# Left-operand blocks of a two-layer decoder trunk stored 132 elements apart instead of 128

## The chip, the cores and the metric

The kernel runs on one core of a Trainium2 chip. The metric is the device time of one execution in microseconds (us).

## The reference: what is computed

Two pre-norm layers on 256 tokens of width 2048, all in float32. Each layer mixes the tokens by attention and then applies a gated feed-forward of 5632 hidden columns:

```python
for layer in range(DEPTH):
    xn = rms_norm(h, norm_mix[layer])
    proj = xn @ w_in                     # 2048 x 5656: queries, keys, values, gates
    o = concat(nsa_attention(...), stick_breaking_attention(...))   # 8 + 8 heads of 128
    h = h + (normed_per_head(o) * g_grp) @ w_out
    xn = rms_norm(h, norm_ffn[layer])
    h = h + (silu(xn @ w_gate) * (xn @ w_up)) @ w_down
return rms_norm(h, norm_final)
```

The weights of both layers are some 420 MB, read once.

## The kernel before

**Three passes.** TensorE multiplies float32 numbers in a format (float32r) that doesn't carry all their bits in one pass. So every operand of the large products is cut into a high part and the rest, and each product is hi x hi + lo x hi + hi x lo. `mm` (L398 to L411) does this for one weight tile: for each block `kt` of 128 rows of the weights, and for each half `t` of the 256 tokens, it issues three matmuls into the accumulator `accs[t]`. The left operand (stationary, loaded into the array ahead of the matmul) is a 128 x 128 block `a` of the high part or `b` of the rest; the right one (moving) is a slice of the weight tile's parts `hi` or `lo`, mostly 512 columns wide:

```python
a = xh[:, kt % 4, t * P:t * P + P]
b = xl[:, kt % 4, t * P:t * P + P]
T.matmul(o, a, hi[:, sl], ...)      # L409
T.matmul(o, a, lo[:, sl], ...)      # L410
T.matmul(o, b, hi[:, sl], ...)      # L411
```

**Weight tiles.** `plan` lists 402 tiles per layer in the order of use. SyncE loads each (128 partitions x up to 1024 columns) into one of 5 slots `raw`; `split_next` has ScalarE round it into `hi` (L165) and VectorE subtract it into `lo` (L166), 4 slots each. A tile of 512-column blocks has two of them, so `hi[:, sl]` starts at the slot or 2,048 bytes behind it. This runs three tiles ahead of the products.

**Left operands.** The normed activations, transposed so that the contracted dimension is on the partitions, are called `xh` and `xl`: tiles of 4 x 256 float32 per partition (4 row blocks, two halves of the tokens each, 4,096 bytes), 5 slots each, in the pool `xp`. `xt_block` (L366) fills them: TensorE transposes into PSUM, VectorE scales, ScalarE writes xh (L380), VectorE xl (L383). They serve the input projection, the output projection and the gate and up products of the feed-forward. The down product has its own, `ah` and `al`, 6 slots each in the pool `fp`, written by `gated` (L929, L930) from the gated activations. Each writer writes four runs of 128 elements, one for each row block, for one half of the tokens.

**Placement.** Pools take their memory one after another: first `xp` (xh, xl), then `wp` (raw, hi, lo), then `sm` (small statistics tiles, 1,408 bytes in all), `tmpp` (three slots of 2,048) and the pool of the stage: the attention's, or `fp` with the slots `sil` of 2,048, in the last layer `gf` of 8,192, and then ah and al. All of this is per partition.

**Other products.** The compressed branch of the attention multiplies `fr` (blocks of 60 columns, 240 bytes apart, L540 and L541) with tiles of 256 columns, in between the input projection's. The first two chunks of the input projection are 280 and 256 columns wide, all others 512.

**The last block of columns** of the last down product is done one half of the tokens after the other. Its ten weight tiles stay in memory for both; for six of them the parts are put into slots of xh and xl (five tiles) and of ah and al (one tile), through `places` (L961 to L969). There the moving operand of a matmul lies in those slots.

**Order.** The order of all instructions is written out by hand: a generator for each piece of work beside the large products does a step at each weight tile.

Of the kernel before, what the change touches and what calls it, by code (L numbers as in the profile page):

```python
# [14 lines left out]
P = 128  # L15
# [10 lines left out]
NEG = -1e30  # L26
SCALE = 128 ** -0.5
EXPLN = "natural_log_exp_and_others"
SILU = "silu_and_others"

# the hidden columns of the feed-forward, in blocks of 512, are worked off in two parts
FF_PARTS = [(0, 6), (6, 11)]

# columns of the constants array
C_ID, C_NEG, C_CNEG, C_COK, C_D1, C_D0, C_MT, C_BM, C_INV, C_END = (
    0, 128, 384, 416, 448, 960, 1472, 1728, 1732, 1748)

# column blocks of the input projection, in the order in which they are computed
IN_CHUNKS = [
# [24 lines left out]
def plan():  # L64
    """The tiles of one layer's weights in the order in which they are used."""

    def tiles(mat, name, cols, k1, k0=0):
        w = sum(c[1] for c in cols)
        step = max(1, min(4, 1024 // w))
        return [Item(mat, name, cols, list(range(k, min(k1, k + step))), k0, k1) for k in range(k0, k1, step)]  # L70

    main = {name: tiles("w_in", name, cols, KT) for name, cols in IN_CHUNKS}
    ck = tiles("w_cmp_k1", "wk", [(0, 256)], 32)
    cv = tiles("w_cmp_v1", "wv", [(0, 256)], 32)
    seq = []
    for name, _ in IN_CHUNKS:
        for j, t in enumerate(main[name]):
            seq.append(t)
            if name == "k" and ck and j >= 1:
                seq.append(ck.pop(0))  # L80
            elif name == "v" and j == 0:
                seq += ck
                ck = []
            elif (name == "v" and j >= 4) or name == "qn0":
                if cv:
                    seq.append(cv.pop(0))
    o = [tiles("w_out", f"o{c}", [(512 * c, 512)], KT) for c in range(4)]
    seq += o[0][:6] + o[1][:6] + o[0][6:] + o[1][6:] + o[2] + o[3]
    for c0, c1 in FF_PARTS:
        for c in range(c0, c1):  # L90
            for m, n in (("w_gate", "g"), ("w_up", "u")):
                seq += tiles(m, f"{n}{c}", [(512 * c, 512)], KT)
        for c in range(4):
            seq += tiles("w_down", f"d{c}", [(512 * c, 512)], 4 * c1, 4 * c0)
    off = 0
    for t in seq:
        t.off = off
        off += P * t.n
    return seq, off


def pi_parts(scale, bits, n):
    """2*pi*scale as n parts of `bits` leading bits each."""
    from fractions import Fraction
    rest = Fraction(2 * 314159265358979323846264338327950288419716939937510582097494459230781640628620899,
                    10 ** 80) * scale
    out = []
    for _ in range(n):
        e = 0
        while rest >= Fraction(2) ** (e + 1):  # L110
            e += 1
        while rest < Fraction(2) ** e:
            e -= 1
        q = Fraction(2) ** (e - bits + 1)
        part = (rest // q) * q
        out.append(float(part))
        rest -= part
    return out
# [3 lines left out]
def trunk(ctx: ExitStack, tc: tile.TileContext, x, positions, cst, gT, gfin, bgate, posT, w2, ws, out):  # L122
# [21 lines left out]

# [1 line left out]
    RAW, AHEAD = 5, 3  # L146
# [30 lines left out]

# [1 line left out]
    active = []  # L179
# [20 lines left out]

# [1 line left out]
    cs = cp.tile([P, C_INV], F32, name="cs")  # L202
# [47 lines left out]

# [1 line left out]
    cc = cp.tile([P, 3, 32], F32, name="cc")  # L252
# [5 lines left out]
    def angles():  # L258
        """positions * inv, brought into [-pi, pi] by an exact subtraction of whole turns."""
        G = nc.gpsimd  # L260
# [49 lines left out]
    def rope(X, tmp, idx, np_=P):  # L310
        """X [np_, n, 128], rotated in place by the tables' row idx."""
        n = X.shape[1]
        cb = cc[:np_, idx:idx + 1, :].to_broadcast([np_, n, 32])
        t = tmp[:np_, :2 * n * 32].rearrange("p (b n d) -> p b n d", b=2, n=n)
        V.tensor_tensor(t[:, 0], X[:, :, 0:32], cb, op=OP.mult)
        V.tensor_tensor(t[:, 1, :, 0:16], X[:, :, 16:32],
                        sn[:np_, idx:idx + 1, 0:16].to_broadcast([np_, n, 16]), op=OP.mult)
        V.tensor_tensor(t[:, 1, :, 16:32], X[:, :, 0:16],
                        sn[:np_, idx:idx + 1, 16:32].to_broadcast([np_, n, 16]), op=OP.mult)
        V.tensor_tensor(X[:, :, 0:32], t[:, 0], t[:, 1], op=OP.add)  # L320

# [1 line left out]
    def rsqrt_a(ss, v, r, count):  # L323
# [12 lines left out]
    class Norm:  # L336
        """1/rms of h per token, gathered block by block."""

# [18 lines left out]

# [1 line left out]
    def new_x():  # L359
        return [None] * 4  # L360

    def xt_alloc(X, c):
        X[c] = (xp.tile([P, 4, S], F32R, tag="xh", name="xh", bufs=5),
                xp.tile([P, 4, S], F32R, tag="xl", name="xl", bufs=5))

    def xt_block(X, c, srcs, g):  # L366
        """[tokens, 512 columns] times g per column, transposed into X[c]."""
        ts = []
# [10 lines left out]
        for t in range(2):  # L379
            A.activation(xh[:, :, t * P:t * P + P], ts[t], AF.Copy)  # L380
        for t in range(2):
            sl = slice(t * P, t * P + P)
            V.tensor_tensor(xl[:, :, sl], ts[t], xh[:, :, sl].bitcast(F32), op=OP.subtract)  # L383

# [13 lines left out]
    def mm(i, accs, X, ts=(0, 1)):  # L398
        """One weight tile: accs[t] += X^T[t] @ W, float32 by three passes."""
        it = seq[i][1]  # L400
        hi, lo = parts[i]
        for j, kt in enumerate(it.kts):
            xh, xl = X(kt)
            sl = slice(j * it.w, (j + 1) * it.w)
            for t in ts:
                o = accs[t][:, :it.w]
                a = xh[:, kt % 4, t * P:t * P + P]
                b = xl[:, kt % 4, t * P:t * P + P]
                T.matmul(o, a, hi[:, sl], start=(kt == it.k0), stop=False)  # L409
                T.matmul(o, a, lo[:, sl], start=False, stop=False)  # L410
                T.matmul(o, b, hi[:, sl], start=False, stop=(kt == it.k1 - 1))  # L411

    # =====================================================================
    norm = Norm()
# [27 lines left out]
    for l in range(DEPTH):  # L442
        g_mix, g_grp, g_ffn = gt[:, 3 * l, :], gt[:, 3 * l + 1, :], gt[:, 3 * l + 2, :]
        flags.clear()
        with ExitStack() as actx:
# [44 lines left out]
            def c_chunk(which, accs):  # L490
                """Tokens of the compressed branch: transposed, cut into blocks, positions added."""
                while "prep" not in flags:
# [105 lines left out]
            def qk_chunk(name, accs):  # L598
                """Queries or keys: scaled, rotated where they are, transposed to [d, token]."""
                sc = rq if name[0] == "q" or name[:2] == "sq" else r  # L600
# [30 lines left out]

# [1 line left out]
            obank = {}  # L633
# [74 lines left out]
            def o_norm(qd, qi, o):  # L708
                """Each head's output over its root mean square."""
                if qd not in on:  # L710
# [44 lines left out]

# [1 line left out]
            def rev(a):  # L757
# [53 lines left out]

# [1 line left out]
            ocmp = {}  # L813
# [42 lines left out]

# [1 line left out]
            spawn(xt_gen(XO, 3, lambda t: on[3][:, t], g_grp, "on3"))  # L858
# [39 lines left out]

# [1 line left out]
        with ExitStack() as fctx:  # L900
# [14 lines left out]
            def gated(c, accs):  # L915
# [3 lines left out]
                yield  # L919
                ah = fp.tile([P, 4, S], F32R, tag="ah", name="ah", bufs=6)  # L920
                al = fp.tile([P, 4, S], F32R, tag="al", name="al", bufs=6)
                for t in range(2):
                    s = sil[c, t]
                    pt = tmp_ps()
                    for j in range(4):
                        T.transpose(pt[:, j * P:(j + 1) * P], s[:, j * P:(j + 1) * P], ident)  # L926
                    sl = slice(t * P, t * P + P)
                    pv = pt.rearrange("p (a b) -> p a b", a=4)
                    A.activation(ah[:, :, sl], pv, AF.Copy)  # L929
                    V.tensor_tensor(al[:, :, sl], pv, ah[:, :, sl].bitcast(F32), op=OP.subtract)  # L930
                    yield
# [65 lines left out]
            else:  # L997
                # the last block of columns: one half of the tokens, whose rows leave beside the other half
                outs = out.rearrange("o (t p) d -> p (o t) d", p=P)
# [87 lines left out]
```

## Time and profile before

| | |
|---|---|
| device time, median of 2 runs | 2322.22 us (both runs) |
| span of the profiled execution, first to last instruction | 2320.4 us |
| TensorE busy | 2301.6 us, 99% of the span |
| VectorE, ScalarE busy | 57%, 47% |
| moved by DMA | 428 MB, mean 185 GB/s |

The profile is of one execution; its own time beside the span is that of the runs shown, which agree to 0.01 us, so about 1.8 us lie around the span. PE are the matmuls, PEld the loads of their left blocks. A matmul's own duration in the trace includes its way through the array, and the next one starts before it ends; how fast TensorE goes is read from the distance between starts.

### The profile page before, as it was taken

Reading aid. Unit: us, or ns where it says so; the run is one execution under the profiler, and the core shown is the slowest. Engines: PE = TensorE matmul, PEld = TensorE weight load, DVE = VectorE, ACT = ScalarE, POOL = GpSimd, SP = SyncE. Lnnn points to the kernel's source line nnn. Section 1 sums busy time; section 2 is a strip of 40 time slices with the busy share of each in tenths; the row PEclk is TensorE's granted clock in tenths of the full one; section 3 lists DMA queues with packets and bytes.
Section 4 is the critical chain, followed back from the end, with each engine's and each line's share of the span. In section 5 each row is a group of like instructions: output and inputs, shape, how many; then the busy total and the mean of one; then the engine's idle time right before and its main releaser. Section 6 shows DMA issues by size and latency. Waiting matters only on the chain.

```text
span 2320.4 us, 28275 instructions
## 1 busy us (share of the span) xinstructions
PE 2301.6 (99%) x10842; PEld 1907.2 (82%) x10842; DVE 1331.5 (57%) x1766; ACT 1082.5 (47%) x1405; POOL 29.0 (1%) x59
## 2 busy tenths in 40 slices
PE   8999999999999999999999999999999999999998
PEld 7888888888888888888888888888888888888886
DVE  6766776655454445445567667765544544544554
ACT  6645554544443344444455455554444433444443
POOL 4000000000000000000000000000000000000000
PEclk9999999999999999999999999999999999999999
DMA  7854456666666666666567434456555555555553
GB/s 251 271 170 129 129 157 195 181 191 189 189 192 185 190 191 186 193 190 184 174 216 251 152 128 145 155 181 210 189 191 191 184 189 190 190 191 191 190 182 136
DMA packets 118824, 428.46 MB, mean 185 GB/s; under 512 B 13424, under 2 KB 13840, under 8 KB 118560
## 3 DMA queue, kind: packets, MB, share of 16 engines
q1 hardware_dynamic: 118464, 426.58, 58.4%
q8 instruction: 85, 1.39, 0.2%
q14 instruction: 51, 0.42, 0.0%
q0 software_dynamic: 224, 0.07, 0.0%
HBM read 424.50 MB, written 2.10 MB: 184 GB/s over the span
## 4 chain that ended last, share of the span: by engine, by line
PE 98%; DVE 1%; ACT 1%; DMA 0%; SPq 0%; issue 0%; ACTq 0%
PE acc L409 30%; PE acc L411 30%; PE acc L410 30%; PE ops L671 1%; PE tps L642 1%; PE tps L926 1%; PE tps L373 1%; PE ops L540 1%; PE ops L541 1%; PE tps L617 1%; PE ops L798 0%; PE tps L663 0%; DMA raw<-in_ws_dram 0%; PE tps L765 0%; PE ops L705 0%; PE tps L680 0%
## 5 line engine op out<-in xcount | busy, mean ns | idle before, releaser
L166 DVE TENSOR_TENSOR lo<-raw,hi 128x1024 fp32r<-128x1024 f32 (+1 forms) x798 | 970.9, 1221 | 825.0 <-ACT hi L165 823.6
L165 ACT ACTIVATE hi<-raw 128x1024 fp32r<-128x1024 f32 (+1 forms) x798 | 836.5, 1054 | 838.6 <-PE acc L411 827.4
L409 PE MATMUL acc<-hi,xh 128*128 128x512 f32 (+2 forms) x2432 | 954.9, 393 | 0.0
L411 PE MATMUL acc<-hi,xl 128*128 128x512 f32 (+2 forms) x2432 | 935.8, 385 | 0.0
L410 PE MATMUL acc<-lo,xh 128*128 128x512 f32 (+2 forms) x2432 | 935.2, 385 | 0.5 <-DVE lo L166 0.5
L411 PEld LDWEIGHTS acc<-hi,xl 128*128 128x128 f32 x2432 | 456.9, 188 | 91.8
L410 PEld LDWEIGHTS acc<-lo,xh 128*128 128x128 f32 x2432 | 457.6, 188 | 89.7 <-issue 3.3
L409 PEld LDWEIGHTS acc<-hi,xh 128*128 128x128 f32 x2432 | 457.5, 188 | 88.7 <-issue 3.3
L409 PE MATMUL acc<-hi,ah 128*128 128x512 f32 x680 | 269.3, 396 | 0.0
L411 PE MATMUL acc<-hi,al 128*128 128x512 f32 x680 | 268.4, 395 | 0.0
L410 PE MATMUL acc<-lo,ah 128*128 128x512 f32 x680 | 268.3, 395 | 0.0
L411 PEld LDWEIGHTS acc<-hi,al 128*128 128x128 f32 x680 | 128.1, 188 | 30.0
L410 PEld LDWEIGHTS acc<-lo,ah 128*128 128x128 f32 x680 | 128.2, 188 | 29.5
L409 PEld LDWEIGHTS acc<-hi,ah 128*128 128x128 f32 x680 | 128.1, 188 | 29.3
L929 ACT ACTIVATE ah<-tps 128x512 fp32r<-128x512 f32 x44 | 26.3, 598 | 83.0 <-PE tps L926 83.0
L930 DVE TENSOR_TENSOR al<-tps,ah 128x512 fp32r<-128x512 f32 x44 | 30.4, 692 | 55.3 <-ACT ah L929 55.3
L380 ACT ACTIVATE xh<-scr 128x512 fp32r<-128x512 f32 x48 | 29.2, 630 | 39.9 <-DVE scr L375 39.8
L665 ACT ACTIVATE pT<-tps 128x256 f32<-128x256 f32 (+1 forms) x32 | 15.7, 490 | 63.4 <-PE tps L663 63.4
L375 DVE TENSOR_TENSOR scr<-tps,gt 128x512 f32<-128x512 f32 x48 | 31.0, 685 | 21.7 <-PE tps L373 21.7
L911 ACT ACTIVATE sil<-acc,nr 128x512 f32<-128x512 f32 x44 | 29.9, 689 | 19.6 <-PE acc L411 19.6
L383 DVE TENSOR_TENSOR xl<-scr,xh 128x512 fp32r<-128x512 f32 x48 | 31.4, 693 | 4.9 <-ACT xh L380 2.9
L540 PE MATMUL ops<-hi,fr 128*60 128x256 f32 x128 | 31.7, 281 | 0.0
(197 smaller groups left out, 976.5 us busy)
## 6 DMA issues: line engine op xcount, KB each, us to landing
raw<-in_ws_dram SPq DMA_DIRECT2D x792, 512.0 KB, 3.6
raw<-in_ws_dram SPq DMA_DIRECT2D x10, 420.0 KB, 4.8
h<-in_x_dram SPq DMA_DIRECT2D x3, 512.0 KB, 8.3
gf<-in_gfin_dram SPq DMA_DIRECT2D x1, 1024.0 KB, 7.8
out_dram<-h SPq DMA_DIRECT2D x4, 256.0 KB, 2.3
out_dram<-h SPq DMA_DIRECT2D x2, 512.0 KB, 3.1
cs<-in_cst_dram SPq DMA_DIRECT2D x1, 802.0 KB, 5.8
h<-in_x_dram SPq DMA_DIRECT2D x2, 256.0 KB, 4.0
```

Source lines behind the costliest of these rows:

```text
L165: A.activation(hi[:, :n], r[:, :n], AF.Copy)
L166: V.tensor_tensor(lo[:, :n], r[:, :n], hi[:, :n].bitcast(F32), op=OP.subtract)
L375: V.tensor_tensor(tv, pt.rearrange("p (a b) -> p a b", a=4), g[:, 4 * c:4 * c + 4, None].to_broadcast([P, 4, P]), op=OP.mult)
L380: A.activation(xh[:, :, t * P:t * P + P], ts[t], AF.Copy)
L383: V.tensor_tensor(xl[:, :, sl], ts[t], xh[:, :, sl].bitcast(F32), op=OP.subtract)
L409: T.matmul(o, a, hi[:, sl], start=(kt == it.k0), stop=False)
L410: T.matmul(o, a, lo[:, sl], start=False, stop=False)
L411: T.matmul(o, b, hi[:, sl], start=False, stop=(kt == it.k1 - 1))
L540: T.matmul(o[:60, :256], fr[:, kt, :], hi[:, sl], start=(kt == 0), stop=False)
L911: A.activation(s, accs[t], AF.Silu, scale=r[:, t:t + 1])
L929: A.activation(ah[:, :, sl], pv, AF.Copy)
L930: V.tensor_tensor(al[:, :, sl], pv, ah[:, :, sl].bitcast(F32), op=OP.subtract)
```

## The change

Each tile of left operands becomes 8 blocks of 132 elements, of which 128 are used: the blocks are 528 bytes apart instead of 512, a slot is 4,224 bytes instead of 4,096, and the four pools of slots (xh, xl, ah, al) grow by 128 bytes per slot. Block 2a + t is row block a, half t of the tokens, in the same order as before. The writers and `mm` take their blocks from a view that leaves the four spare elements out; nothing reads or writes those. The six weight tiles that are put into these slots at the end keep their own shape of 4 x 256 elements.

```diff
+XS = 132
...
+    def slices(tl):
+
+        return tl.rearrange("p (a t) b -> p a t b", t=2)[:, :, :, :P]
+
     def xt_alloc(X, c):
-        X[c] = (xp.tile([P, 4, S], F32R, tag="xh", name="xh", bufs=5),
-                xp.tile([P, 4, S], F32R, tag="xl", name="xl", bufs=5))
+        X[c] = (slices(xp.tile([P, 8, XS], F32R, tag="xh", name="xh", bufs=5)),
+                slices(xp.tile([P, 8, XS], F32R, tag="xl", name="xl", bufs=5)))
...
         for t in range(2):
-            A.activation(xh[:, :, t * P:t * P + P], ts[t], AF.Copy)
+            A.activation(xh[:, :, t], ts[t], AF.Copy)
         for t in range(2):
-            sl = slice(t * P, t * P + P)
-            V.tensor_tensor(xl[:, :, sl], ts[t], xh[:, :, sl].bitcast(F32), op=OP.subtract)
+            V.tensor_tensor(xl[:, :, t], ts[t], xh[:, :, t].bitcast(F32), op=OP.subtract)
...
-                a = xh[:, kt % 4, t * P:t * P + P]
-                b = xl[:, kt % 4, t * P:t * P + P]
+                a = xh[:, kt % 4, t]
+                b = xl[:, kt % 4, t]
...
-                ah = fp.tile([P, 4, S], F32R, tag="ah", name="ah", bufs=6)
-                al = fp.tile([P, 4, S], F32R, tag="al", name="al", bufs=6)
+                ah = slices(fp.tile([P, 8, XS], F32R, tag="ah", name="ah", bufs=6))
+                al = slices(fp.tile([P, 8, XS], F32R, tag="al", name="al", bufs=6))
...
-                    sl = slice(t * P, t * P + P)
                     pv = pt.rearrange("p (a b) -> p a b", a=4)
-                    A.activation(ah[:, :, sl], pv, AF.Copy)
-                    V.tensor_tensor(al[:, :, sl], pv, ah[:, :, sl].bitcast(F32), op=OP.subtract)
+                    A.activation(ah[:, :, t], pv, AF.Copy)
+                    V.tensor_tensor(al[:, :, t], pv, ah[:, :, t].bitcast(F32), op=OP.subtract)
```

## Rows read from the trace of the kernel before

**Rows 1.** The page: span, busy time of the engines, granted TensorE clock in 40 slices.

```profile
span 2320.4 us, 28275 instructions
...
PE 2301.6 (99%) x10842; PEld 1907.2 (82%) x10842; DVE 1331.5 (57%) x1766; ACT 1082.5 (47%) x1405; POOL 29.0 (1%) x59
...
PEclk9999999999999999999999999999999999999999
```

**Rows 2.** The page: chain that ended last, shares of the span by engine.

```profile
PE 98%; DVE 1%; ACT 1%; DMA 0%; SPq 0%; issue 0%; ACTq 0%
```

**Rows 3.** Groups of TensorE matmuls by line and shape: count, busy us, mean ns.

```profile
line engine op names shapes xcount | busy us, mean ns | idle before us <-releasers
L409 PE MATMUL acc<-hi,xh 128*128 128x512 f32 x2304 | 917.4, 398 | 0.0
...
L409 PE MATMUL acc<-hi,ah 128*128 128x512 f32 x680 | 269.3, 396 | 0.0
...
L409 PE MATMUL acc<-xh,ah 128*128 128x512 f32 x20 | 7.9, 394 | 0.0
...
L409 PE MATMUL acc<-ah 128*128 128x512 f32 x4 | 1.6, 391 | 0.0
```

**Rows 4.** Windows (length, busy us, count), TensorE alone: four stretches of one kind.

```profile
core 0: us, PE busy (x), PEclk, DMA share, GB/s
1760.16:1800.86 40.70, 40.70 (x182) 1.00 0.58 194
1849.24:1977.37 128.13, 128.13 (x554) 1.00 0.57 189
28.99:40.39 11.40, 11.40 (x98) 1.00 0.85 307
1166.44:1178.73 12.29, 12.29 (x99) 1.00 0.42 139
```

**Rows 5.** Timeline, feed-forward of layer 1: matmul (PE), load (PEld): start, duration us.

```profile
1770.04 0.39 PE L410 MATMUL acc<-lo,xh 128*128 128x512 f32 x1
...
1770.04 0.19 PEld L411 LDWEIGHTS acc<-hi,xl 128*128 128x128 f32 x1
```

**Rows 6.** Timeline of TensorE, last block of columns of the last projection.

```profile
2287.80 0.39 PE L409 MATMUL acc<-xh,ah 128*128 128x512 f32 x1
...
2290.58 0.39 PE L409 MATMUL acc<-ah 128*128 128x512 f32 x1
...
2291.94 0.40 PE L409 MATMUL acc<-hi,ah 128*128 128x512 f32 x1
```

**Rows 7.** Timeline of TensorE: two tiles of lines 540 and 541; a restart.

```profile
98.82 0.28 PE L540 MATMUL ops<-hi,fr 128*60 128x256 f32 x1
...
99.63 0.28 PE L541 MATMUL ops<-lo,fr 128*60 128x256 f32 x1
...
106.18 0.28 PE L540 MATMUL ops<-hi,fr 128*60 128x256 f32 x1
...
107.00 0.28 PE L541 MATMUL ops<-lo,fr 128*60 128x256 f32 x1
...
1300.18 0.39 PE L410 MATMUL acc<-lo,xh 128*128 128x512 f32 x1
...
1302.49 0.39 PE L411 MATMUL acc<-hi,xl 128*128 128x512 f32 x1
```

**Rows 8.** The page: groups of ScalarE and VectorE that write the left operands.

```profile
L929 ACT ACTIVATE ah<-tps 128x512 fp32r<-128x512 f32 x44 | 26.3, 598 | 83.0 <-PE tps L926 83.0
...
L380 ACT ACTIVATE xh<-scr 128x512 fp32r<-128x512 f32 x48 | 29.2, 630 | 39.9 <-DVE scr L375 39.8
...
L383 DVE TENSOR_TENSOR xl<-scr,xh 128x512 fp32r<-128x512 f32 x48 | 31.4, 693 | 4.9 <-ACT xh L380 2.9
```

**Rows 9.** The chain in order of time, joint of input and output projection, layer 0.

```profile
319.05 1.14 ACT xh L380 x2
```

## The prediction

> **What bounds the kernel now.** I read the page first. TensorE is busy 99% of a span of 2320.4 us at the full clock (1.00, that is 2.4 GHz) [rows 1], and the chain that ended last is TensorE's for 98% [rows 2]. No stage waits for data for long, so the only way to another time is another pace of TensorE: how far apart matmuls start. The groups by shape give the counts: each of the lines 409, 410 and 411 has 2304 matmuls of 512 columns whose left operand is xh or xl, and 680 + 20 + 4 whose left operand is ah or al [rows 3]. Over the three lines that is 6,912 of the first kind (X) and 2,112 of the second (A), 9,024 in all. One nanosecond on each is 9 us, 0.4% of the run.
>
> Then I looked for the pace itself, in stretches in which nothing but one kind of matmul runs [rows 4]. A window's count includes what began just before it and ends in it, so I take the matmuls of the loop. The 180 X matmuls from 1760.16 start 40.70/179 = 227.4 ns apart. The 552 A matmuls from 1849.24 start 128.13/551 = 232.5 ns apart. The 96 matmuls of 256 columns from 28.99 take 11.40/95 = 120.0 ns, the 96 of 280 columns from 1166.44 take 12.29/95 = 129.4 ns. From 256 to 512 columns of the X kind a column costs (227.4 - 120.0)/256 = 0.42 ns, one clock of 2.4 GHz. So 512 columns are 214.8 ns, 280 are 117.5, 256 are 107.4, and what is above that I call the extra: 12.6 ns for X, 12.6 for the 256 columns, 11.9 for the 280, 17.7 for A. The extra is the prey: 6,912 x 12.6 + 2,112 x 17.7 = 124 us, 5% of the run.
>
> Why is A 5 ns slower than X? Not the stage: in the last block of columns, where the left operand is ah throughout, 12 matmuls whose moving tile lies in a slot of the xh pool take (2290.58 - 2287.80)/12 = 231.7 ns and the next 6, whose moving tile lies in a slot of the ah pool, (2291.94 - 2290.58)/6 = 226.7 [rows 6]. Same left operand, same instructions, other addresses. And while a matmul streams its moving tile, the next left block is being loaded: the load for line 411 starts at 1770.04, with the matmul of line 410 [rows 5]. So two reads of SBUF run side by side, and their distance in the memory matters. The program fixes that distance. Slots of xh, xl, raw, hi and lo are 4,096 bytes, allocated in a row, and blocks are 512 bytes apart, halves of a moving tile 2,048: every X block is at distance 0 from its moving tile, modulo 512. Before the ah pool lie the small statistics tiles, 1,408 bytes in the allocation, and slots of 2,048 and more: A is at 384, modulo 512. In the 6 matmuls above both come from the ah pool: distance 0 again, and X's pace again.
>
> **The change part by part.** It adds and removes no instruction, no transfer and no wait. It moves each block by 528 bytes instead of 512, each slot by 4,224 instead of 4,096. Modulo 512 the blocks of a slot then stand at 0, 16, ... 112 and the slots at 0, 128, 256, 384 from one another: X and A alike go through all multiples of 16, and the distance is another one every one to three matmuls. What is wanted is one number, the mean pace p over mixed distances. The sum is
>
> time = 2322.2 + 6,912 x (p - 227.4 ns) + 2,100 x (p - 232.5 ns),
>
> with 2,100 for A since 12 are at distance 0 already; the end stays where TensorE's sequence ends. The break-even is p = 228.6.
>
> No row of before has full blocks of 128 columns at mixed distances under 512 moving columns, so p is bounded from the nearest ones:
> - Lower: the matmuls of lines 540 and 541, whose left blocks are 240 bytes apart and so do go through the multiples of 16. Two tiles of them: 0.81/7 = 115.7 ns and 0.82/7 = 117.1 [rows 7], mean 116.4, an extra of 9.0. But their blocks have 60 columns. Taken as it is: p = 214.8 + 9.0 = 223.8.
> - Upper: the same extra in proportion to the columns loaded, 9.0 x 128/60 = 19.2: p = 234.0.
> - Nearer: the 280 columns, with blocks of 128 columns and three distances (1,120 bytes from one slice of the moving tile to the next), extra 11.9: p = 226.7.
> - Nearer: X itself, just after other work has come between: ten matmuls from 1300.18 take (1302.49 - 1300.18)/10 = 231.0 [rows 7] at distance 0, an extra of 16.2, and only then does the pace of 227 set in. So X's 227.4 is a rhythm into which a long run at one distance settles, and mixed distances allow no settling. With A's 17.7 the unsettled extra at 512 columns is 17.0.
>
> The 280 columns are right in the mixing and wrong in the length, the restart and A are right in the length and wrong in the mixing. I take the middle, 14.4: p = 229.2. X loses 6,912 x 1.8 = 12.4 us, A gains 2,100 x 3.3 = 6.9 us; the sum is +5.5 us. From the profiled execution's span of 2320.4 with 1.8 us around it (the runs' median is 2322.2), that gives 2328 us. At the lower bound the sum is -43 us, at the upper +49.
>
> The writers of these tiles keep their element counts; only the step between their four runs of 128 grows. ScalarE takes 630 ns for one, VectorE 693, 598 ns ScalarE for ah [rows 8], 48 + 44 of each. I cost this at nothing: TensorE works off other blocks meanwhile. Where that cover is missing, at the joint of input and output projection, two of the writes stand in the chain with 1.14 us [rows 9], once a layer; a tenth more on them would be 0.2 us in all, and nothing says that they could get faster. The tiles of hi, lo and raw keep their size and their distances to each other, and the queues see the same order of transfers.
>
> **A rule that speaks against any effect.** Rows 6 show two paces for one left operand at two addresses, 231.7 and 226.7 ns. The Trainium skill (TensorE: Matmul & The Clock Gate, Step-by-step: what each phase is for) says that the engine has two independent read ports, one for the moving operand and one for loading, and that loading the next weights takes nothing from the running matmul. By that rule the time would stay at 2322 us; the trace's 5 ns of difference disagree, so I keep it as a rival only.
>
> **The rivals.**
> - The distance doesn't matter, and rows 6 differ for another reason, such as what else was being written then. Then X stays at 227.4 and A at 232.5, and the time is 2322 us. For it: an A tile always comes with its stage. Against it: the switch within one stage, at once with the slot. Chance 0.08.
> - X loses its rhythm altogether: every new distance starts the unsettled pace anew, p from 231.0 to 234.0, time 2344 to 2371. For it: the restart at 231.0 and A at 232.5, both at 512 columns. Against it: the 280 columns, which never settle either and pay less than X. It ends slower from p = 228.6 on, and slower by over 2% from p = 233.8. Chance 0.20, of which 0.05 beyond 2%.
> - The mixed distances mostly let the two reads pass each other, p below 227.5, time below 2312. For it: 226.7 from the 280 columns and 223.8 from lines 540 and 541. Against it: those load fewer columns, or stream fewer. 2% needs p under 223.4; with no extra at all it would be 2322 - 124 = 2198 us. Chance 0.22, of which 0.10 beyond 2%.
>
> **How the numbers follow.** The forecast, p between 227.5 and 231.0, 2312 to 2344 us, has 0.50, and its likeliest value is 2328. 2% of the run, about what a measurement can tell from no change, is 46 us: 2276 and 2369. Faster by over 2% is 0.10, slower 0.05, within 2% is 0.85. The range leaves out about 0.11 below (p under 224.3: 2285 us) and 0.07 above (p over 232.4: 2356 us).
>
> **What would show it.** In the profile after, with the counts unchanged, the X run of 180 matmuls and the A run of 552 should have the same pace within 2 ns, near 229: some 41.0 us for the first (40.7 before), 126.3 for the second (128.1 before). The single steps should no longer repeat but go with the block. The 256 columns should move with X. If A stays at 232.5 and X at 227.4, the distance is not the cause. If X goes to 231 and over, the rhythm was worth more than I gave it; if both fall under 227, mixing is better than any one distance. I would be wrong in kind if TensorE began to wait, that is, if its busy share fell below 99%.

## The result: 2351.35 us, 1.25% slower

The changed kernel takes 2351.35 us, the kernel before 2322.22: a ratio of 1.0125, with a 95% interval of 1.0096 to 1.0155. That is 29.1 us more. It lies above 2312 to 2344 us, to which the forecast gave a chance of 0.50, and inside the wider range from 2285 to 2356.

The page of the changed kernel (span, busy time, chain) against [rows 1, 2]:

```profile
span 2349.5 us, 28275 instructions
...
PE 2330.4 (99%) x10842; PEld 1907.2 (81%) x10842; DVE 1331.7 (57%) x1766; ACT 1082.6 (46%) x1405; POOL 29.1 (1%) x59
...
PE 98%; DVE 0%; ACT 0%; DMA 0%; SPq 0%; issue 0%; ACTq 0%
```

The same number of instructions, TensorE as busy as before at 99%, and the chain TensorE's for 98%. TensorE's busy time is 28.8 us longer (2301.6 before), which is nearly all of the loss. No wait came or went: the span without TensorE's busy time is 18.8 us before and 19.1 after. So it is the pace.

Groups by line and shape of the changed kernel (L414 is what L409 was), against [rows 3]:

```profile
L414 PE MATMUL acc<-hi,xh 128*128 128x512 f32 x2304 | 927.9, 403 | 0.0
...
L414 PE MATMUL acc<-hi,ah 128*128 128x512 f32 x680 | 269.4, 396 | 0.0
```

The first line of the three has 10.5 us more with xh (917.4 before), and 0.1 more with ah. Only one of the two kinds of matmul became slower. Windows of the changed kernel (length, busy us, count), the same four runs of matmuls as in [rows 4]:

```profile
core 0: us, PE busy (x), PEclk, DMA share, GB/s
2143.83:2185.45 41.62, 41.62 (x182) 1.00 0.59 190
1873.87:2001.83 127.96, 127.96 (x555) 1.00 0.57 189
29.27:40.50 11.23, 11.23 (x97) 1.00 0.83 303
1181.09:1193.41 12.32, 12.32 (x98) 1.00 0.43 150
```

From first to last start these are 41.62/179 = 232.5 ns for X (227.4 before), 127.96/551 = 232.2 for A (232.5 before), 11.23/95 = 118.2 for the 256 columns (120.0 before) and 12.32/95 = 129.7 for the 280 (129.4 before). X now has A's pace. The runs of X and of A follow other work, and the first step alone takes 315 to 318 ns in all four; that adds 0.5 ns to a mean over 179 steps and 0.2 to one over 551. By the starts in the trace, to the nanosecond, the steps from the 41st on are 226.7 ns for X and 232.4 for A before, and 232.1 for both after. In the changed kernel they range from 226 to 240 and come again in the same order to within 2 ns, every 96 matmuls for X and every 48 for A: they go with the block, as the prediction said.

Behind an interruption (timeline, the same place in layer 1 as the restart in [rows 7], ten matmuls apart):

```profile
1316.06 0.39 PE L415 MATMUL acc<-lo,xh 128*128 128x512 f32 x1
...
1318.39 0.39 PE L416 MATMUL acc<-hi,xl 128*128 128x512 f32 x1
```

2.33/10 = 233.0 ns, where it was 231.0: there X had little to lose. The gate and up products, which run long without interruption, have 2 x 11 x 16 x 6 x 2 = 4,224 of the 6,912 X matmuls; at 5.1 ns each that is 21.5 us. A gave back 2,100 x 0.3 = 0.6. The other 2,688 X matmuls, in the interrupted input and output projections, are left with about 8 us, 3 ns each, between the 2.0 of the restart and 5.1.

### The profile page after: what moved, and what is told of

The parts are those of the page before. It is cut to its first block, busy times and chain, and to the rows that moved or that the text cites. A ratio compares the mean times of both kernels' runs of the same rounds, so it can differ in the third digit from the quotient of the medians.

```text
span 2349.5 us, 28275 instructions
## 1 busy us (share of the span) xinstructions
PE 2330.4 (99%) x10842; PEld 1907.2 (81%) x10842; DVE 1331.7 (57%) x1766; ACT 1082.6 (46%) x1405; POOL 29.1 (1%) x59
## 4 chain that ended last, share of the span: by engine, by line
PE 98%; DVE 0%; ACT 0%; DMA 0%; SPq 0%; issue 0%; ACTq 0%
PE acc L414 30%; PE acc L415 30%; PE acc L416 30%; PE ops L676 1%; PE tps L647 1%; PE tps L931 1%; PE tps L379 1%; PE ops L545 1%; PE ops L546 1%; PE tps L622 1%; PE ops L803 0%; PE tps L668 0%; DMA raw<-in_ws_dram 0%; PE tps L770 0%; PE ops L710 0%; PE tps L685 0%
## 5 line engine op out<-in xcount | busy, mean ns | idle before, releaser
L414 PE MATMUL acc<-hi,xh 128*128 128x512 f32 (+2 forms) x2432 | 965.1, 397 | 0.0
L415 PE MATMUL acc<-lo,xh 128*128 128x512 f32 (+2 forms) x2432 | 945.5, 389 | 0.4 <-DVE lo L168 0.4
L414 PEld LDWEIGHTS acc<-hi,xh 128*128 128x128 f32 x2432 | 457.7, 188 | 97.7 <-issue 3.3
L414 PE MATMUL acc<-hi,ah 128*128 128x512 f32 x680 | 269.4, 396 | 0.0
L414 PEld LDWEIGHTS acc<-hi,ah 128*128 128x128 f32 x680 | 127.7, 188 | 28.8
```

## The experiments

The theory: the pace depends on the distance between the block being loaded and the tile being streamed, and X stood at a good distance. Its first rival: the writers, or the longer slots, cost the time. The second: it is the mixing alone, and any constant distance is good. A third: it is what the other engines read and write at the same time.

### Half of the change each

```diff
# e1: the changed kernel, ah and al as before
-                ah = slices(fp.tile([P, 8, XS], F32R, tag="ah", name="ah", bufs=6))
+                ah = view(fp.tile([P, 4, S], F32R, tag="ah", name="ah", bufs=6))
# e2: the changed kernel, xh and xl as before
-        X[c] = (slices(xp.tile([P, 8, XS], F32R, tag="xh", name="xh", bufs=5)),
+        X[c] = (view(xp.tile([P, 4, S], F32R, tag="xh", name="xh", bufs=5)),
```

`view` gives the blocks of a tile of 4 x 256; al and xl are treated in the same way.

> Of the change the xh and xl slots alone (blocks 132 apart); ah and al as before. Distance theory: X mixes its distances and loses its rhythm, 232.5 ns between starts; A stays at 384 modulo 512 and at 232.5. Time 2351 us, all of the 29 us of the change. Rival (the writers or the longer slots of ah and al cost the time): 2322 to 2330 us.

> Of the change the ah and al slots alone; xh and xl as before. Distance theory: X keeps 227.4 ns at distance 0, A goes from one unsettled pace to another, 232.5 to 232.2 ns. Time 2321 to 2323 us, no change. Rival (the writers or the longer slots of ah and al cost the time): 2340 us or more.

Measured: xh and xl alone 2351.69 us (ratio 1.0127, 1.0112 to 1.0142), ah and al alone 2321.39 (0.9996, 0.9986 to 1.0005). Windows of the X run of 180 and the A run of 552, first with xh and xl alone, then with ah and al alone:

```profile
2144.42:2186.04 41.62, 41.62 (x182) 1.00 0.59 190
1874.28:2002.40 128.12, 128.12 (x554) 1.00 0.57 189
```

```profile
2115.85:2156.52 40.67, 40.67 (x183) 1.00 0.57 194
1848.95:1976.92 127.97, 127.97 (x555) 1.00 0.57 189
```

41.62/179 = 232.5 and 128.12/551 = 232.5 in the first, 40.67/179 = 227.2 and 127.97/551 = 232.3 in the second. All of the loss is X's, and longer slots of ah and al with their writers cost nothing. The halves add up: 29.6 - 0.7 = 28.9 of 29.1 us. Both outcomes are the theory's.

### The distance alone, blocks 128 apart as before

```diff
# e3: the kernel before, 128 bytes ahead of ah and al
+            fctx.enter_context(tc.tile_pool(name=f"gap{l}", bufs=1)).tile([P, 32], F32, name="gapa")
             fp = fctx.enter_context(tc.tile_pool(name=f"fp{l}", bufs=1))
# e4: the kernel before, 128 bytes between the pools of left operands and of weight parts
     xp = ctx.enter_context(tc.tile_pool(name="xp", bufs=5))
+    ctx.enter_context(tc.tile_pool(name="gap", bufs=1)).tile([P, 32], F32, name="gap")
     wp = ctx.enter_context(tc.tile_pool(name="wp", bufs=4))
```

> The kernel before, with 128 spare bytes per partition ahead of the pool of ah and al, so that A too stands at distance 0 modulo 512 from its moving tiles. Distance theory: A falls from 232.5 to X's 227.4 ns, 2,100 x 5.1 ns = 10.7 us less, 2311.5 us. Rival (A is slower because of its stage, not its place): 232.5 ns, 2322 us.

> The kernel before, with 128 spare bytes between the pool of xh, xl and the pool of raw, hi, lo: blocks 128 elements apart as before, X at the constant distance 384 modulo 512 at which A stands. Distance theory: X goes to A's 232.5 ns, 6,912 x 5.1 = 35 us at most, about 2350 us as in the changed kernel. Rival (it is the mixing alone that costs; any constant distance lets the pace settle at 227): 2322 us.

Measured: A at distance 0 gives 2310.55 us (0.9951, 0.9934 to 0.9968), 0.5% faster than the kernel before; X at 384 gives 2358.17 (1.0155, 1.0139 to 1.0170), slower than the changed kernel. The second is 8 us more than was expected, and 36 us above the kernel before where the expectation had 35 at most. Windows of the X run of 180 and the A run of 552, first with A at 0, then with X at 384:

```profile
2107.09:2147.80 40.71, 40.71 (x183) 1.00 0.57 194
1843.05:1968.08 125.03, 125.03 (x555) 1.00 0.58 194
```

```profile
2149.61:2191.45 41.84, 41.84 (x182) 1.00 0.56 189
1878.21:2006.85 128.64, 128.64 (x554) 1.00 0.57 188
```

With A at 0 it runs at 125.03/551 = 226.9 ns instead of 232.5; with X at 384 it runs at 41.84/179 = 233.7 instead of 227.4. No block was stored farther from the next one, so a spacer of 128 bytes alone moves a pace by as much as the change did. The rival that any constant distance is good falls: 384 is constant. The last block of columns of that kernel shows it once more within one stage (timeline; L410 is the first of the three lines):

```profile
2315.92 0.39 PE L410 MATMUL acc<-hi,ah 128*128 128x512 f32 x1
...
2319.41 0.39 PE L410 MATMUL acc<-xh,ah 128*128 128x512 f32 x1
...
2326.23 0.39 PE L410 MATMUL acc<-ah 128*128 128x512 f32 x1
```

In the kernel before, a moving tile in a slot of xh had 231.7 ns there [rows 6]. The spacer has moved the weight parts and ah by 128 bytes and left xh where it was, so now the moving tile from the xh pool is at distance 0: 30 matmuls from 2319.41 take 6.82/30 = 227.3 ns, and the 15 ahead of them, with moving tiles `hi` and `lo`, 3.49/15 = 232.7. The fast and the slow tile have changed places.

The third rival falls by the order of the steps. At distance 0 they repeat every 3 matmuls (226, 227, 227 ns) and in the A run of the kernel before every 7 (228 to 241 ns), to within 1 ns once a run has settled, while ScalarE and VectorE come round to the same work once in a weight tile, which is 12 matmuls.

### Is it the distance or the block's own place?

```diff
# e8: as e3, and 160 bytes ahead of all operands
+    ctx.enter_context(tc.tile_pool(name="gap0", bufs=1)).tile([P, 40], F32, name="gap0")
     xp = ctx.enter_context(tc.tile_pool(name="xp", bufs=5))
```

> The kernel before with 160 spare bytes ahead of all pools of operands and 128 ahead of ah and al: every left block starts elsewhere in a line of 512 bytes than in the run with A at 0, and both X and A are at distance 0 as there. Distance theory: 227.4 ns for both, 2310.5 us as in that run. Rival (it is the block's own start that counts, not its distance from the moving tile): another pace than 227, 2340 us or more.

Measured: 2310.46 us, a single run. Windows of the X run of 180 and the A run of 552:

```profile
2107.34:2148.03 40.69, 40.69 (x182) 1.00 0.59 194
1843.32:1968.33 125.01, 125.01 (x554) 1.00 0.58 194
```

40.69/179 = 227.3 and 125.01/551 = 226.9 ns, as with A at 0 without the shift. The block's own start doesn't matter, its distance does.

### Other constant distances

Five kernels, two of them further below, put X and the A of either layer at constant distances of their own. Three do it by spacers of other lengths at the places of e3 and e4 (in e5: 64 bytes at the place of e4, 160 and 192 ahead of ah in layers 0 and 1; in e6: 192, 96 and 224; in e7: 256, 32 and 64):

> The kernel before with spare bytes: 64 between the pools of xh, xl and of raw, hi, lo (X at 448 modulo 512, constant), ahead of ah and al 160 in layer 0 (A at 32) and 192 in layer 1 (A at 64). If only distance 0 lets the pace settle at 227: all three paces 230 to 234 ns, time 2340 to 2360 us. Rival (384 is the bad distance, most others are as good as 0): X and A near 227, 2312 us.

> As the run before it, other constant distances modulo 512: X at 320, A at 480 in layer 0 and 96 in layer 1. If only distance 0 settles: 230 to 234 ns everywhere, 2340 to 2360 us. Rival (a distance with a pace under 226 exists, as the single tiles of lines 540 and 541 with 113 ns hint): one of the three paces under 226 ns.

> As the run before it: X at 256, A at 416 in layer 0 and 448 in layer 1, modulo 512. If the pattern repeats every 256 bytes: X at 227.4 as at 0, time 2322 us within 3. If it repeats every 512 or more: X at 230 to 234, 2340 to 2360 us.

Measured, a single run each: 2334.02, 2362.26 and 2320.43 us. Windows of e5, e6 and e7: the X run of 180, the A runs of 552 in layer 0 and in layer 1.

```profile
2127.08:2168.15 41.07, 41.07 (x182) 1.00 0.58 192
703.12:831.76 128.64, 128.64 (x554) 1.00 0.64 188
1858.21:1986.86 128.65, 128.65 (x555) 1.00 0.56 188
```

```profile
2153.45:2195.30 41.85, 41.85 (x182) 1.00 0.57 189
712.95:841.61 128.66, 128.66 (x555) 1.00 0.63 188
1881.50:2010.66 129.16, 129.16 (x555) 1.00 0.57 187
```

```profile
2116.20:2156.90 40.70, 40.70 (x182) 1.00 0.58 194
700.69:829.34 128.65, 128.65 (x554) 1.00 0.63 188
1850.91:1977.12 126.21, 126.21 (x555) 1.00 0.58 192
```

X at 256 has 40.70/179 = 227.4 ns, exactly what it has at 0; X and A at 448, one distance for both kinds, have 41.07/179 = 229.4 and 126.21/551 = 229.1; X at 320 has 41.85/179 = 233.8, A at 64 has 128.65/551 = 233.5. So 0 agrees with 256 and 64 with 320: the pattern repeats every 256 bytes, as the first expectation of e7 had it. That 230 to 234 holds for all but 0 was wrong for 192 modulo 256. The time of e5 was 6 us below what had been expected of it, that of e6 2 us above.

For distances that are odd multiples of 16 the tiles got longer slots:

```diff
# e9: as e3, slots of 4352 bytes, the tile 240 bytes into them (e10: 16)
-        X[c] = (xp.tile([P, 4, S], F32R, tag="xh", name="xh", bufs=5),
+        sl = slice(60, 60 + 1024)
+        X[c] = (xp.tile([P, 1088], F32R, tag="xh", name="xh", bufs=5)[:, sl].rearrange("p (a b) -> p a b", a=4),
...
```

The same is done to xl, and to ah and al with 208 bytes in layer 0 and 176 in layer 1 (e10: 48 and 144).

> Blocks 128 elements apart as before, slots of 4352 bytes (17 times 256) in which the tile starts behind some spare bytes, so that the distance is constant modulo 256: X at 240, A at 208 in layer 0 and 176 in layer 1. If 0 is the one distance that settles well: X above 228 ns, time 2325 us or more. Rival (208, at which single matmuls of lines 540 and 541 were shortest, or 240 or 176 beats 0): a pace under 226.5 ns in its stage.

> As the run before it: X at 16, A at 48 in layer 0 and 144 in layer 1, modulo 256. If 0 is the one distance that settles well: X above 228 ns, time 2325 us or more. Rival (a distance beside 0 is as good or better): a pace of 227 ns or less in its stage.

Measured, a single run each: 2319.70 and 2334.53 us. Windows of the same three runs in e9 and in e10; the last three rows of e10 are other uninterrupted runs of X matmuls, one of 60 in the input projection, one of 204 in the gate and up products and another of 60 in the input projection:

```profile
2115.09:2155.77 40.68, 40.68 (x183) 1.00 0.59 194
700.12:827.96 127.84, 127.84 (x554) 1.00 0.64 189
1849.01:1975.83 126.82, 126.82 (x555) 1.00 0.59 191
```

```profile
2128.41:2169.09 40.68, 40.68 (x182) 1.00 0.60 194
704.96:833.62 128.66, 128.66 (x555) 1.00 0.64 187
1859.46:1988.11 128.65, 128.65 (x554) 1.00 0.58 188
1448.49:1462.34 13.85, 13.85 (x63) 1.00 0.69 228
1988.34:2035.71 47.37, 47.37 (x205) 1.00 0.57 189
1275.40:1288.88 13.48, 13.48 (x62) 1.00 0.64 213
```

X at 240 has 40.68/179 = 227.3 ns in the run of 180 and the kernel's time is 2319.7, against the expectation. X at 16 has 227.3 too in the run of 180 (40.68/179). But in the first run of 60 it has 13.85/59 = 234.7, and the kernel is 12 us slower than before, some 2 of them by A at 233.5. The length of the run isn't what decides: the run of 204 has 47.37/203 = 233.3, and the other run of 60 has 13.48/59 = 228.5.

The steps in the trace show what does differ. Behind its first steps each run repeats a fixed cycle, and at 16 there are at least two: 226, 227, 227 ns in the runs of 180 and the second run of 60, and 232 to 235 ns, with a mean of 233.3, in the run of 204 and the first run of 60. At 240 there is a second one too, of 226 and 229 ns with a mean of 228.3, in all four runs of 60. And at 384 X in e4 alternates between 229 and 238 ns (or 230 and 237) in the run of 180 above, but has the 7 steps of A in the kernel before in a run of 192 (window of e4; 44.47/191 = 232.8 ns):

```profile
1601.76:1646.23 44.47, 44.47 (x195) 1.00 0.62 206
```

The runs of 60 have the same cycle at the same place in both layers, so what stands ahead of a run seems to choose it; no experiment changed that alone. At 0 and 256 every uninterrupted run of 48 X matmuls and more comes to 226, 227, 227 ns.

No distance beat 0. All paces of the runs of 180 and 552, first step included, in ns:

| distance modulo 256 | 0 | 16 | 32 | 48 | 64 | 96 | 128 |
|---|---|---|---|---|---|---|---|
| X | 227.4 | 227.3 | | | 233.8 | | 233.7 |
| A | 226.9 | | 233.5 | 233.5 | 233.5 | 234.4 | 232.5, 233.5 |

| distance modulo 256 | 144 | 160 | 176 | 192 | 208 | 224 | 240 |
|---|---|---|---|---|---|---|---|
| X | | | | 229.4 | | | 227.3 |
| A | 233.5 | 233.5 | 230.2 | 229.1 | 232.0 | 233.5 | |

The mean over these 14 distances (of two values, their mean) is 231.6 ns. The changed kernel, which goes through all multiples of 16, has 232.2 to 232.5. So it has little more than the average of the distances that were tried, and X before had one of the three best. That X and A differ by 0.5 ns at distance 0 is for the most part the first step: from the 41st on both have 226.7.

## Why the prediction held, and where it was off

**That the pace is all.** Right: same counts, no new wait, TensorE at 99%, and its busy time grew by 28.8 of the 29.1 us.

**That the distance of two reads sets the pace.** Right, and shown: a spacer that changes addresses alone gives A 5.6 ns or takes 6.3 from X, and a shift of everything changes nothing. It isn't quite the whole: at 16, 240 and 384 one distance has two cycles. That the reads of the load and of the stream hold each other up inside the memory is still only an inference: no run took one of the two away. Distances modulo 512 were more than was needed: it is 256.

**That X and A get one common pace.** Right: 232.5 and 232.2 ns, within the 2 ns that were given, and 232.1 for both from the 41st step on.

**The size of that pace.** Here the sum failed: p was taken as 229.2, the middle of 226.7 (the 280 columns) and of the unsettled 231.8 (an extra of 17.0). Measured were 232.5 and 232.2. X lost 5.1 ns each in the long runs instead of 1.8, A gained 0.3 instead of 3.3. The wrong step is the weight on the 280 columns. They went from 129.4 to 129.7, and the 256 columns even fell from 120.0 to 118.2, while 512 columns lost 5.1: short moving tiles don't follow the same curve, so that row bore on the mixing no more than the others. The sign that the 256 columns should move with X failed with it. The rows of full length, the restart and A, came nearly right, but by luck: each is the pace of one distance and not of a mixture. The rival that was given 0.20, X at 231 to 234 and a time of 2344 to 2371, came true in its numbers and not in its mechanism (see the rhythm below); the likeliest case with its 2312 to 2344 did not. A slip beside it: p = 224.3 gives 2283.6 us by the formula, not 2285.

**X's pace before.** 227.4 holds in long runs only. With the measured paces the formula gives 6,912 x 5.1 - 2,100 x 0.3 = 34.6 us, 5.5 more than were lost, since the interrupted projections were slower than 227.4 before. That would be 2356.8 us, above the 2356 at which the range ends: the time lies inside it by this second error, which is luck.

**"A rhythm into which a long run at one distance settles."** Half right. There is such a settling: 231.0 behind an interruption and 226.7 later. But a constant distance alone doesn't bring that pace: at 32 to 160 the long runs stay at 232.5 to 234.4. And that mixed distances allow no settling is wrong: the steps of the changed kernel recur, every 96 and every 48 matmuls. X became slower not because its rhythm was lost, but because most distances are bad ones. What mixing adds to the average of those tried is under 1 ns.

**The rule of two ports.** The Trainium skill's sentence (TensorE: Matmul & The Clock Gate, Step-by-step: what each phase is for) that loading the next weights takes no read bandwidth of SBUF from the running matmul would have left the time at 2322 us. With the spacers the same instructions ran at 226.9 to 234.4 ns; the measurement decides against that time, for this format and these shapes.

**The writers, costed at nothing.** Right: with longer slots for ah and al alone the time stayed within 0.1%, and the writers of xh and xl take 630 and 693 ns each in the changed kernel, as in [rows 8].

**What stays open.** Why these distances are good and not others, and what chooses between two cycles at one distance: at 16, at 240, and at 384, where A has 232.5 ns in the kernel before and 233.5 in e4. Distances 80 and 112 were not tried.

## What to carry to other kernels

Where loads of the stationary operand run under the matmuls of a full TensorE, look at the distance between starts, not at the durations, and compare it between stages that do the same work on other tiles: here 5 ns between X and A pointed at the memory's layout before anything was changed. Choose pool sizes so that the stationary blocks stand at one good distance from the moving tiles (here 0 modulo 256 bytes, blocks 512 apart and slots of 4,096; 16 and 240 are as good in some runs only), rather than spread them: padding gave about the average of all distances, and that is only a gain for blocks that stood at a worse one. A spacer of 128 bytes ahead of ah and al, with the blocks 128 elements apart as before, gives 2310.55 us: 0.5% faster than the kernel before and 1.7% than the changed one.

## What the runs showed of the hardware

In float32r, with 512 moving columns and a load of 128 columns under each matmul, the time between matmuls at the full clock went from 226.9 to 234.4 ns by the distance of the two addresses, in a pattern that repeats every 256 bytes, with the minimum around 0 (240, 0 and 16: 226.9 to 227.4 in the runs of 180 and 552) and a second, shallower one at 176 to 192 (229.1 to 230.2). These paces are settled cycles of steps: after an interruption the same distance 0 costs 231.0 ns at first, and one distance can have two cycles, at 16 one of 226.7 ns and one of 233.3. And with 256 moving columns distance 0 was not the best: 120.0 ns there, 118.2 in the changed kernel.
